# Experts in the order of their token counts, three of them as 64 slots with high and low halves side by side

## Chip, cores, metric

One core of a Trainium2 chip runs the whole program. The metric is the device time of one execution in microseconds (us); the runs of the kernel before give a median.

## What is computed

Two layers of a hybrid trunk on 256 latent tokens and 256 context tokens, then a final norm. The change lies in the second layer's expert part alone:

```python
logits = (x @ router_w).astype(F32)
top_val, top_idx = lax.top_k(logits, TOP_K)          # 2 of 8 experts
gates = jax.nn.softmax(top_val, axis=-1)
def swiglu(x, w1, w3, w2):
    return (jax.nn.silu(x @ w1) * (x @ w3)) @ w2
y = jax.ops.segment_sum(yb * buf_gate[:, None].astype(yb.dtype), buf_tok, num_segments=n_tok + 1)
```

256 tokens choose two experts each, so 512 rows are spread over 8 experts of width 1024 to 2816 to 1024, all in fp32. With the inputs used here the reference's router gives experts 0 to 7 the counts 46, 68, 65, 64, 79, 75, 55 and 60.

## The kernel before

`stage_two` holds the expert part. A token's slot within an expert is the number of tokens before it with the same expert (`rank`). `place` builds for every expert the 0/1 matrix `G` (256 tokens by 128 slots), `gather` multiplies the tokens' rows by it for a pair of experts, `back` transposes it into `GT`, and `scatter` brings an expert's rows back to their tokens and adds them to `xlat`. If an expert had more than 128 tokens (`nmax > P`), the whole loop `experts` would run once more on the rest.

`experts` goes through the experts 0 to 7. Each has 33 weight chunks of 1 MB (128 partitions by 2048 values): 22 for w1 and w3 (two for each of 11 steps `b`), 11 for w2. `raws` gives a chunk one of nine places of its own (`NQ + NX`) and, for two early ones, a place borrowed from another tile; SP's queue issues the loads in the order of the program and waits for a place to come free. `wsplit` makes two fp32r halves out of a chunk: ScalarE (ACT) casts it to the high part `wh` (L1056), VectorE (DVE) subtracts to get the low part `wl` (L1057), 1024 columns at a time, into four places each (`NSW`). An fp32 product is then three fp32r products on TensorE (PE):

```python
pe.matmul(p, xh, wH, start=(kt == 0), stop=False)
pe.matmul(p, xh, wL, start=False, stop=False)
pe.matmul(p, xl, wH, start=False, stop=(kt == KT - 1))
```

(L1203 to L1205 for w1 and w3, the same in L1253 to L1255 for w2), each with 128 slots as the stationary operand and 512 weight columns streaming: 12 a chunk. After a step's 24 products ACT takes the silu (L1213), DVE multiplies (L1214), PE transposes two tiles of 128x128 (L1217), and ACT and DVE split the result into `gh` and `gl` (L1223, L1224). Two PSUM banks `h` take turns between steps. At the end of a half of w2, ACT and DVE scale and split the rows (L1258, L1259).

The order of instructions on each engine is fixed when the program is built, by a scheduler that moves them away from the order of the code; at run time every engine goes through its own list and waits where an operand is missing.

## Time and profile before

| | us |
|---|---|
| median of 3 runs | 1838.36 |
| lowest, highest run | 1838.15, 1841.06 |
| span of the profiled execution, first to last instruction | 1837.7 |
| TensorE busy in it | 1776.0 (97%) |
| VectorE busy | 1413.4 (77%) |
| ScalarE busy | 1058.8 (58%) |
| mean rate of the DMA engines | 223 GB/s |

The profiled execution's own time is its span, 1837.7 us, and what lies around the span, which the profile does not hold. A busy time is the union of an engine's instructions; a share over the whole span averages stages of different kinds, and the expert loop is the last 800 us or so. Pipelined products overlap in the records, so the distance from one start to the next tells more than one record's length.

### The profile page before, as it was taken

How to read it: one execution, taken by the hardware profiler on the slowest of the kernel's cores; microseconds unless marked ns; L12 is line 12 of the kernel's file. 1: busy time of each engine (PE TensorE's matmuls, PEld its weight loads, DVE VectorE, ACT ScalarE, POOL GpSimd, SP SyncE). 2: the span in 40 equal slices, each digit the busy share in tenths (PEclk: the TensorE clock that was granted, in tenths of full speed). 3: DMA queues.
4: the chain of work that ended last, by engine and by line, in shares of the span. 5: the costliest groups of instructions: out<-in, count | busy, mean ns of one | idle time of the engine just before them, and what ended most of it. 6: DMA issues, size and time to landing. Idle time of an engine off the chain costs nothing.

```text
span 1837.7 us, 24441 instructions
## 1 busy us (share of the span) xinstructions
PE 1776.0 (97%) x8925; PEld 1403.1 (76%) x8925; DVE 1413.4 (77%) x2437; ACT 1058.8 (58%) x1648; POOL 3.0 (0%) x9
## 2 busy tenths in 40 slices
PE   6999999999999999899999899999999999999997
PEld 4776666778888888687768788888787878878786
DVE  4657757679986333677767899999889998999896
ACT  3455556533222222365456687878777777777775
POOL 0000000000000000000000000000000000000000
PEclk9999999989999999899999899999999999999998
DMA  9643211227785332331315789989998999989991
GB/s 302 224 143 126 81 45 51 72 93 241 232 309 204 92 97 78 125 101 55 104 50 184 290 332 354 367 333 354 341 345 334 353 346 346 358 330 367 341 368 61
DMA packets 82863, 410.09 MB, mean 223 GB/s; under 512 B 8912, under 2 KB 18640, under 8 KB 48944
## 3 DMA queue, kind: packets, MB, share of 16 engines
q1 hardware_dynamic: 82000, 406.62, 61.8%
q8 instruction: 72, 1.18, 0.3%
q0 software_dynamic: 304, 1.29, 0.2%
q10 hardware_dynamic: 432, 0.55, 0.1%
q14 instruction: 55, 0.45, 0.1%
HBM read 407.38 MB, written 1.05 MB: 222 GB/s over the span
## 4 chain that ended last, share of the span: by engine, by line
PE 91%; DVE 3%; ACT 2%; DMA 2%; issue 1%; SPq 0%; DVEq 0%; ACTq 0%; POOLq 0%
PE ah L1204 9%; PE ah L1203 9%; PE ah L1205 9%; PE ay L1254 4%; PE ay L1255 4%; PE ay L1253 4%; PE atr L1217 1%; PE axgp L1164 1%; DMA aw<-ada 1%; PE asc L1267 1%; PE nk L87 1%; PE nk L85 1%; PE cq L85 1%; PE nk L86 1%; PE cq L87 1%
## 5 line engine op out<-in xcount | busy, mean ns | idle before, releaser
L1057 DVE TENSOR_TENSOR am_1wl<-am_1w,am_1wh 128x1024 fp32r<-128x1024 f32 (+1 forms) x178 | 210.9, 1210 | 25.2 <-ACT am_1wh L1056 21.6
L1057 DVE TENSOR_TENSOR am_0wl<-am_0w,am_0wh 128x1024 fp32r<-128x1024 f32 (+1 forms) x178 | 209.8, 1206 | 3.8 <-ACT am_0wh L1056 3.2
L1056 ACT CAST am_0wh<-am_0w 128x1024 fp32r<-128x1024 f32 (+1 forms) x178 | 180.2, 1044 | 15.3 <-PE ah L1205 8.1
L1056 ACT CAST am_1wh<-am_1w 128x1024 fp32r<-128x1024 f32 (+1 forms) x178 | 179.1, 1036 | 9.1 <-PE ah L1205 7.7
L1205 PE MATMUL ah<-am_0wh,axl 128*128 128x512 f32 x352 | 142.5, 405 | 0.0
L1204 PE MATMUL ah<-am_0wl,axh 128*128 128x512 f32 x352 | 140.5, 399 | 0.0
L1203 PE MATMUL ah<-am_0wh,axh 128*128 128x512 f32 x352 | 139.4, 396 | 0.0
L1204 PE MATMUL ah<-am_1wl,axh 128*128 128x512 f32 x352 | 138.7, 394 | 0.0
L1203 PE MATMUL ah<-am_1wh,axh 128*128 128x512 f32 x352 | 138.0, 392 | 0.0
L1205 PE MATMUL ah<-am_1wh,axl 128*128 128x512 f32 x352 | 137.5, 391 | 0.0
L249 DVE CUSTOM_DVE_ANT_0 junk<-awr,crow,sp 128x1024 f32<-128x1024 f32 x80 | 102.6, 1283 | 12.9 <-DMA awr<-adr 11.6
L1213 ACT ACTIVATE as<-ah 128x256 f32<-128x256 f32 x88 | 34.0, 386 | 88.2 <-PE ah L1205 88.2
L1203 PEld LDWEIGHTS ah<-am_1wh,axh 128*128 128x128 f32 x352 | 66.1, 188 | 14.8
L1205 PEld LDWEIGHTS ah<-am_1wh,axl 128*128 128x128 f32 x352 | 66.1, 188 | 13.8
L1204 PEld LDWEIGHTS ah<-am_1wl,axh 128*128 128x128 f32 x352 | 66.2, 188 | 13.7 <-DVE am_1wl L1057 0.4
L1204 PEld LDWEIGHTS ah<-am_0wl,axh 128*128 128x128 f32 x352 | 66.4, 189 | 13.2 <-DVE am_0wl L1057 0.9
L1203 PEld LDWEIGHTS ah<-am_0wh,axh 128*128 128x128 f32 x352 | 66.6, 189 | 12.5 <-ACT axh L1169 0.4
L1205 PEld LDWEIGHTS ah<-am_0wh,axl 128*128 128x128 f32 x352 | 66.4, 189 | 11.3
L1214 DVE TENSOR_TENSOR as<-as,ah 128x256 f32<-128x256 f32 x88 | 36.4, 414 | 4.6 <-ACT as L1213 4.6
L1224 DVE TENSOR_TENSOR agl<-atr,agh 128x256 fp32r<-128x256 f32 x88 | 36.8, 418 | 1.9 <-ACT agh L1223 1.2
L1223 ACT CAST agh<-atr 128x256 fp32r<-128x256 f32 x88 | 32.7, 372 | 5.5 <-PE atr L1217 5.1
L1217 PEld LDWEIGHTS atr<-ck,as 128*128 128x128 f32 x176 | 23.5, 139 | 13.7 <-DVE as L1214 4.3
(6122 smaller groups left out, 4884.8 us busy)
## 6 DMA issues: line engine op xcount, KB each, us to landing
am_0w<-m SPq DMA_DIRECT2D x88, 1024.0 KB, 5.7
am_1w<-m SPq DMA_DIRECT2D x88, 1024.0 KB, 6.1
awr<-adr SPq DMA_DIRECT2D x56, 512.0 KB, 4.5
aw<-ada SPq DMA_DIRECT2D x24, 512.0 KB, 4.6
aw<-ada SPq DMA_DIRECT2D x32, 256.0 KB, 6.0
av_0w<-m SPq DMA_DIRECT2D x8, 1024.0 KB, 5.4
av_1w<-m SPq DMA_DIRECT2D x8, 1024.0 KB, 5.8
av_2w<-m SPq DMA_DIRECT2D x8, 1024.0 KB, 5.0
```

The lines of the kernel that those rows point to most:

```text
L85: pe.matmul(ps, a[0], b[0], start=first, stop=False)
L249: ins = dve.tensor_tensor_reduce(out=junk, in0=w, in1=rows[v], op0=OP.mult, op1=OP.add, scale=1.0, scalar=sp[:, l, b:b + 1], accum_out=mod ...
L1056: act.copy(h[:, c], r)
L1057: dve.tensor_tensor(l[:, c], r, f32(h[:, c]), op=OP.subtract)
L1203: pe.matmul(p, xh, wH, start=(kt == 0), stop=False)
L1204: pe.matmul(p, xh, wL, start=False, stop=False)
L1205: pe.matmul(p, xl, wH, start=False, stop=(kt == KT - 1))
L1217: pe.transpose(tr[:, u * P:(u + 1) * P], s[:, u * P:(u + 1) * P], ident)
L1224: dve.tensor_tensor(gl, trv, f32(gh), op=OP.subtract)
L1253: pe.matmul(yq, gh, wH, start=(f == 0), stop=False)
L1254: pe.matmul(yq, gh, wL, start=False, stop=False)
L1255: pe.matmul(yq, gl, wH, start=False, stop=(f == NF - 1))
```

## The change

The program counts the tokens of each expert on the chip (`order`), ranks experts 1 to 7 by count and visits them in an order of eight places: place 0 stays expert 0, places 1, 3 and 5 get those with the three smallest counts (`RANKS`). SP reads the seven numbers into registers (`values_load`), and the loads of places 1 to 7 take their address from one (`weights`). `G`, gates and ranks are permuted to places.

Places 1, 3 and 5 (`NARROW`) hold at most 64 tokens. Their stationary tile has the 64 tokens' high parts in columns 0 to 63 and the low parts in columns 64 to 127, so two products (by `wH` and `wL`) do what three did (`narrow`). Of their 33 chunks, five (`WHOLE`) are not split: one plain fp32 product streams the raw chunk. A step's result then has the high parts' sums in partitions 0 to 63 and the low parts' in 64 to 127: ACT copies the bank out (`ev`) and a product with `fold` adds the lower half to the upper. Silu, multiplication and transposes go over 64 partitions or columns. Experts are gathered as 0, then 1 and 2, 3 and 4, 5 and 6, then 7. The gates' arithmetic is called at the same place; `place` for the others comes after `order`. A second pass runs if a place overflows its cap of 64 or 128.

```diff
@@ -49,8 +49,14 @@
-C_ID, C_ONE, C_IOTA, C_SEL, C_TIE = 0, 128, 256, 384, 392
-N_CK = 456
+C_ID, C_ONE, C_IOTA, C_SEL, C_TIE, C_SIG = 0, 128, 256, 384, 392, 456
+N_CK = 488
+RANKS = (0, 1, 4, 2, 5, 3, 6, 7)
+NARROW = (1, 3, 5)
+CAP = tuple(64 if s in NARROW else 128 for s in range(8))
+WHOLE = (3, 10, 16, 23, 29)
 T_R, T_M0, T_M1, T_UP, T_LO, T_BO, T_K = 0, 512, 896, 1280, 1408, 1536, 1664
...
@@ -1039,12 +1045,14 @@
-        def wsplit(src, name):
+        def wsplit(src, name, split=True):
             rt_ = raws(nchunk[0], name + "w")
...
             nchunk[0] += 1
+            if not split:
+                return [(rt_[0][:, :1024], None), (rt_[0][:, 1024:], None)]
             res = []
...
@@ -1058,20 +1066,29 @@
         def unit(ws, k, c0=0, n=512):
-            return [t[:, k % 2 * 512 + c0:k % 2 * 512 + c0 + n] for t in ws[k // 2]]
+            return [t if t is None else t[:, k % 2 * 512 + c0:k % 2 * 512 + c0 + n] for t in ws[k // 2]]
+        def narrow(p, x, w, first, last):
+            if w[1] is None:
+                pe.matmul(p, f32(x), w[0], start=first, stop=last)
+            else:
+                pe.matmul(p, x, w[0], start=first, stop=False)
+                pe.matmul(p, x, w[1], start=False, stop=last)
...
         oh1, oh2, asg, gate, rank, rk2, t1 = (rt[:, i] for i in range(7))
+        asgp, rankp, gatep = oh1, oh2, t1
         lg = plog
...
@@ -1111,26 +1128,25 @@
-        def place(rk, e0, e1):
+        def place(rk, ag, e0, e1, nm):
             for e in range(e0, e1):
                 for tt in range(2):
-                    ins = dve.tensor_scalar(G[tt][:, e, :], iota, rk[:, tt, e:e + 1], asg[:, tt, e:e + 1],
+                    g = G[tt][:, e, :]
+                    i = iota
+                    if nm == "a" and e in NARROW:
+                        g = g.rearrange("p (a b) -> p a b", a=2)
+                        i = ck[:, None, C_IOTA:C_IOTA + 64].to_broadcast([P, 2, 64])
+                    ins = dve.tensor_scalar(g, i, rk[:, tt, e:e + 1], ag[:, tt, e:e + 1],
                                             op0=OP.is_equal, op1=OP.mult)
...
-        with tc.issue_after(place(rank, 0, 2).ins):
+        with tc.issue_after(place(rank, asg, 0, 1, "a").ins):
             for p_ in parts[HL:]:
...
         def gates():
...
@@ -1144,82 +1160,157 @@
             dve.tensor_tensor(gate, gate, t1, op=OP.add)
-            dve.tensor_scalar(rk2, rank, -128.0, None, op0=OP.add)
-            return ci
-        cnti = []
+        def order():
...
+            for tt in range(2):
+                pe.matmul(pr[:, 16:24], on, lot[:, tt, :], start=(tt == 0), stop=(tt == 1))
+            dve.tensor_copy(cnt, pr[:, 16:24])
+            dve.tensor_tensor(key, cnt, row[0], op=OP.mult)
+            dve.tensor_tensor(key, key, row[1], op=OP.add)
+            dve.tensor_tensor(w1_, key[:, None, :].to_broadcast(sq8), key[:, :, None].to_broadcast(sq8), op=OP.is_lt)
+            dve.tensor_reduce(pos, w1_, AX.X, OP.add)
+            dve.tensor_tensor(hot, pos[:, None, :].to_broadcast(sq8), row[2][:, :, None].to_broadcast(sq8), op=OP.is_equal)
+            dve.tensor_tensor(w1_, hot, i8[:, None, :].to_broadcast(sq8), op=OP.mult)
+            dve.tensor_reduce(idx, w1_, AX.X, OP.add)
+            dve.tensor_copy(oi[:, :NEXP], idx)
...
+            for dst, src in ((rankp, rank), (asgp, asg), (gatep, gate)):
+                by_place(dst, src)
+            dve.tensor_tensor(w1_, hot, cnt[:, None, :].to_broadcast(sq8), op=OP.mult)
+            dve.tensor_reduce(over, w1_, AX.X, OP.add)
...
+            fold = whole.tile([P, P], F32R, tag="before", name="fold")
+            dve.tensor_copy(fold[:, :64], ident[:, 64:])
+            dve.tensor_scalar(fold[:, 64:], ident[:, :64], 0.0, None, op0=OP.mult)
+            return oi, fold
+        oi, regs = [], []
         def experts(rk, nm):
...
+            def gather(e0, ne):
...
+                            if e0 + i in thin:
+                                dve.scalar_tensor_tensor(h_[:, m:c], pv[:, m:c], sh, f32(h_[:, a:m]), op0=OP.add,
+                                                         op1=OP.subtract)
...
             def slots(e):
-                if e == 0 and nm == "a":
-                    cnti.append(gates())
                 pg = bank("t", 2, f"{nm}pg{e}")
                 for tt in range(2):
-                    pe.matmul(pg[:, :1], f32(G[tt][:, e, :]), gate[:, tt, e:e + 1], start=(tt == 0), stop=(tt == 1))
+                    pe.matmul(pg[:, :1], f32(G[tt][:, e, :]), gatep[:, tt, e:e + 1], start=(tt == 0), stop=(tt == 1))
                 dve.tensor_copy(gs[:, e:e + 1], pg[:, :1])
...
                 tr = bank("t", 2, f"{nm}gt{e}")
-                for u in range(2):
-                    for tt in range(2):
-                        pe.transpose(tr[:, u * NL + tt * P:u * NL + (tt + 1) * P], f32(G[tt][:, e + u, :]), ident)
-                act.copy(GT[:, e:e + 2, :], tr.rearrange("p (e t) -> p e t", e=2))
+                for tt in range(2):
+                    pe.transpose(tr[:, tt * P:(tt + 1) * P], f32(G[tt][:, e, :]), ident)
+                act.copy(GT[:, e, :], tr[:, :NL])
+            def weights(key, e, *c):
+                return I[key][(e, *c)] if e == 0 else I[key][(bass.ds(regs[e], 1), *c)].rearrange("o p c -> (o p) c")
...
                 if e == 0:
-                    xg = gather(0)
-                    place(rk, 2, NEXP)
-                o = (e % 2) * P
+                    xg = gather(0, 1)
+                o = 0 if e == 0 else (e - 1) % 2 * P
+                slim = e in thin
+                n_ = 64 if slim else P
                 gts = []
...
                     for kh in range(2):
-                        ws = wsplit(I["m13"][e, b, kh], f"{nm}m{e}_{b}_{kh}")
+                        ws = wsplit(weights("m13", e, b, kh), f"{nm}m{e}_{b}_{kh}", not (slim and 2 * b + kh in WHOLE))
                         for k4 in range(4):
...
                             xh, xl = xg[0][:, kt, o:o + P], xg[1][:, kt, o:o + P]
+                            if slim:
+                                narrow(p, xh, (wH, wL), kt == 0, kt == KT - 1)
+                                continue
                             pe.matmul(p, xh, wH, start=(kt == 0), stop=False)
...
                             pe.matmul(p, xl, wH, start=False, stop=(kt == KT - 1))
-                    if b == SLB:
+                    if slim:
+                        ev = cp.tile([P, 512], F32, tag="pm", bufs=3, name=f"{nm}ev{e}_{b}").bitcast(F32R)
+                        act.copy(ev, p)
+                        pe.matmul(p, oi[1], ev, start=False, stop=True, skip_group_check=True)
+                    if nm == "a" and e == 0 and b == SLB:
+                        gates()
+                        oi.extend(order())
+                        regs.extend([0] + [nc.values_load(oi[0][0:1, s_:s_ + 1], engines=[mybir.EngineType.SP], min_val=0,
+                                                          max_val=NEXP - 1) for s_ in range(1, NEXP)])
+                    if nm == "a" and e == 0 and b == SLB + 1:
+                        place(rankp, asgp, 1, NEXP, nm)
+                    if b == SLB + 1:
                         slots(e)
-                    if e == 0 and BK <= b < BK + 4:
-                        back(2 * b - 2 * BK)
+                    if b == BK:
+                        back(e)
                     if b == 1 and late:
                         late.pop()()
-                    s = cp.tile([P, 512], F32, tag="pm", bufs=3, name=f"{nm}s{e}_{b}")[:, :256]
-                    act.activation(s, p[:, :256], AF.Silu)
-                    dve.tensor_tensor(s, s, p[:, 256:], op=OP.mult)
+                    s = cp.tile([P, 512], F32, tag="pm", bufs=3, name=f"{nm}s{e}_{b}")[:n_, :256]
+                    act.activation(s, p[:n_, :256], AF.Silu)
+                    dve.tensor_tensor(s, s, p[:n_, 256:], op=OP.mult)
...
+                    if slim:
+                        act.copy(gh[:, :, :64], trv)
+                        dve.tensor_tensor(gh[:, :, 64:], trv, f32(gh[:, :, :64]), op=OP.subtract)
+                        gts.append((gh, None))
+                        continue
...
@@ -1227,16 +1318,16 @@
                     hh, f = divmod(u, NF)
-                    if u == 16 and e % 2 == 1 and e + 1 < NEXP:
-                        xg = gather((e + 1) // 2)
+                    if u == 16 and e % 2 == 0 and e + 1 < NEXP:
+                        xg = gather(e + 1, min(2, NEXP - 1 - e))
                     if u % 4 == 0:
-                        ws = wsplit(I["m2"][e, u // 4], f"{nm}v{e}_{u // 4}")
+                        ws = wsplit(weights("m2", e, u // 4), f"{nm}v{e}_{u // 4}", not (slim and 22 + u // 4 in WHOLE))
                     if e == NEXP - 1 and u == NF:
...
@@ -1248,8 +1339,11 @@
                             f = u_ % NF
+                            wH, wL = unit(ws, u_ % 4, q * n, n)
+                            if slim:
+                                narrow(yq, gts[f // 2][0][:, f % 2, :], (wH, wL), f == 0, f == NF - 1)
+                                continue
                             gh, gl = gts[f // 2][0][:, f % 2, :], gts[f // 2][1][:, f % 2, :]
-                            wH, wL = unit(ws, u_ % 4, q * n, n)
                             pe.matmul(yq, gh, wH, start=(f == 0), stop=False)
...
@@ -1304,8 +1398,8 @@
         experts(rank, "a")
-        nmax = nc.values_load(cnti[0][0:1, 0:1], min_val=0, max_val=NL)
-        with tc.If(nmax > P):
+        nmax = nc.values_load(oi[0][0:1, NEXP:NEXP + 1], min_val=0, max_val=NL)
+        with tc.If(nmax > 0):
             experts(rk2, "b")
...
@@ -1320,6 +1414,7 @@
     ck[:, C_TIE:C_TIE + NEXP * NEXP] = np.where(e[None] < e[:, None], 0, np.where(e[None] > e[:, None], 1.2e-38, 3.0e38)).ravel()
+    ck[:, C_SIG:C_SIG + 32] = np.concatenate([[0] + [8] * 7, [-1, 1, 2, 3, 4, 5, 6, 7], RANKS, CAP])[None]
     ck[:, C_SEL:C_SEL + 8] = (i[:, None] % 32) == np.arange(8)[None]
```

How the built order moves is seen at two places. The first is PE in the first of the three places (`ah` is a step's bank, the number behind it the step; `wh`, `wl` the weights' parts; `aev` the copied bank; `atr` the transposes). Before, in the second expert, the nine products that follow step 2's last one and its two gate products, and then the transposes of step 2:

```order
L1203 MATMUL ah_3_9796<-am_3_0wh_9799,axh_8643 128x512
L1204 MATMUL ah_3_9796<-am_3_0wl_9800,axh_8643 128x512
L1205 MATMUL ah_3_9796<-am_3_0wh_9799,axl_8644 128x512
L1203 MATMUL ah_3_9796<-am_3_0wh_9799,axh_8643 128x512
L1204 MATMUL ah_3_9796<-am_3_0wl_9800,axh_8643 128x512
L1205 MATMUL ah_3_9796<-am_3_0wh_9799,axl_8644 128x512
L1203 MATMUL ah_3_9796<-am_3_0wh_9803,axh_8643 128x512
L1204 MATMUL ah_3_9796<-am_3_0wl_9804,axh_8643 128x512
L1205 MATMUL ah_3_9796<-am_3_0wh_9803,axl_8644 128x512
L1217 MATMUL atr_2_9791<-ck,as_2_9788 128x128 x2
```

Now, from the last product of step 2 on:

```order
L1079 MATMUL ah_2_9850<-am_2_1wl_9876,axh_9516 128x512
L1078 MATMUL ah_3_9898<-am_3_0wh_9901,axh_9516 128x512
L1079 MATMUL ah_3_9898<-am_3_0wl_9902,axh_9516 128x512
L1078 MATMUL ah_3_9898<-am_3_0wh_9901,axh_9516 128x512
L1079 MATMUL ah_3_9898<-am_3_0wl_9902,axh_9516 128x512
L1078 MATMUL ah_3_9898<-am_3_0wh_9905,axh_9516 128x512
L1079 MATMUL ah_3_9898<-am_3_0wl_9906,axh_9516 128x512
L1078 MATMUL ah_3_9898<-am_3_0wh_9905,axh_9516 128x512
L1283 MATMUL ah_2_9850<-aev_2_9887,fold 128x512
L1079 MATMUL ah_3_9898<-am_3_0wl_9906,axh_9516 128x512
L1078 MATMUL ah_3_9898<-am_3_1wh_9919,axh_9516 128x512
```

Two products stand where three stood, the fold of step 2 comes seven products after its last one, and the transposes of step 2 (two of 128x64) eight products after the fold.

The second place is DVE in the first expert, step 3 to step 4 (`am_3_1wl` and `am_4_0wl` are low parts of the chunks of steps 3 and 4, `ordw` the work area of `order`, `oi` the numbers for SP). Before:

```order
L1057 TENSOR_TENSOR am_3_1wl_8928<-am_3_1w,am_3_1wh_8927 128x1024
L1146 TENSOR_TENSOR rt<-rt 128x16
L1214 TENSOR_TENSOR as_2_8894<-as_2_8894,ah_2_8825 128x256
L1180 COPY gslot<-apg_8890 128x1
L1057 TENSOR_TENSOR am_3_1wl_8932<-am_3_1w,am_3_1wh_8931 128x1024
L1057 TENSOR_TENSOR am_4_0wl_8959<-am_4_0w,am_4_0wh_8958 128x1024
L1224 TENSOR_TENSOR agl_0_8769<-atr_2_8897,agh_0_8768 128x256
L1057 TENSOR_TENSOR am_4_0wl_8963<-am_4_0w,am_4_0wh_8962 128x1024
```

Now, from the last split of step 3:

```order
L1065 TENSOR_TENSOR am_3_1wl_9006<-am_3_1w,am_3_1wh_9005 128x1024
L1183 TENSOR_TENSOR ordw<-ordw,ck 128x64
L1315 TENSOR_TENSOR agl_0_8755<-atr_2_8971,agh_0_8754 128x256
L1184 TENSOR_TENSOR ordw<-ordw,ck 128x64
L1190 TENSOR_TENSOR ordw<-ordw,rt 128x128
L1185 TENSOR_REDUCE ordw<-ordw 128x8
L1191 TENSOR_REDUCE rt<-ordw 128x16
L1186 CAST oi<-ordw 128x8
L1195 TENSOR_TENSOR ordw<-ordw 128x64
L1190 TENSOR_TENSOR ordw<-ordw,rt 128x128
L1196 TENSOR_REDUCE ordw<-ordw 128x8
L1191 TENSOR_REDUCE rt<-ordw 128x16
```

Before, two splits of successive chunks stand side by side there. Now 34 instructions stand between the last split of step 3 and the first of step 4: 17 of `order`, 14 that build `G` for the other seven experts (these stood ahead of step 1 before), the copy of the gates and two that stood there before too.

## Rows read from the trace of the kernel before

**Rows 1.** The page: span, and busy time of each engine.

```profile
span 1837.7 us, 24441 instructions
PE 1776.0 (97%) x8925; PEld 1403.1 (76%) x8925; DVE 1413.4 (77%) x2437; ACT 1058.8 (58%) x1648; POOL 3.0 (0%) x9
```

**Rows 2.** The page: the chain that ended last, by line.

```profile
PE ah L1204 9%; PE ah L1203 9%; PE ah L1205 9%; PE ay L1254 4%; PE ay L1255 4%; PE ay L1253 4%; PE atr L1217 1%; PE axgp L1164 1%; DMA aw<-ada 1%; PE asc L1267 1%; PE nk L87 1%; PE nk L85 1%; PE cq L85 1%; PE nk L86 1%; PE cq L87 1%
```

**Rows 3.** The chain in time: one place, two experts apart (start us, us, what).

```profile
1304.81 0.47 PE ay L1253 x2
...
1504.91 0.47 PE ay L1253 x2
```

**Rows 4.** Busy time by stretch: those two experts.

```profile
core 0: us, PE busy (x) PEld busy (x) DVE busy (x) ACT busy (x) POOL busy (x), PEclk, DMA share, GB/s
...
1304.80:1504.90 200.10, 197.46 (x910) 160.46 (x909) 181.04 (x207) 147.98 (x188) 0.00 (x0) 1.00 0.94 346
```

**Rows 5.** Waits in those two experts: us in total, times, longest.

```profile
PE ay L1254 <- DVE av_7wl L1057: 2.4, 2, 1.2
...
PEld atr L1217 <- DVE as L1214: 0.6, 1, 0.6
```

**Rows 6.** Timeline of PE, two products twelve apart (start us, us).

```profile
1170.44 0.39 PE L1203 MATMUL ah<-am_1wh,axh 128*128 128x512 f32 x1
...
1173.19 0.39 PE L1203 MATMUL ah<-am_0wh,axh 128*128 128x512 f32 x1
```

**Rows 7.** Plain fp32 products of 512 columns: one tile's row, one of the chain.

```profile
L772 PE MATMUL krr<-krs,ctB x2: 587/588/588, 863.1 to 863.5; 64*128 64x512 f32 x2
...
915.86 0.86 PE ma1010s L376 x2
```

**Rows 8.** The chain: four transposes of 128 columns.

```profile
1081.46 0.44 PE agt L1186 x4
```

**Rows 9.** Groups by line and shape, those two experts, DVE.

```profile
L1057 DVE TENSOR_TENSOR am_1wl<-am_1w,am_1wh 128x1024 fp32r<-128x1024 f32 x44 | 52.1, 1221 | 8.1 <-ACT am_1wh L1056 8.1
...
L1224 DVE TENSOR_TENSOR agl<-atr,agh 128x256 fp32r<-128x256 f32 x22 | 9.2, 418 | 0.2 <-ACT agh L1223 0.2
L1214 DVE TENSOR_TENSOR as<-as,ah 128x256 f32<-128x256 f32 x22 | 9.1, 414 | 2.0 <-ACT as L1213 2.0
```

**Rows 10.** The same for ACT.

```profile
L1056 ACT CAST am_0wh<-am_0w 128x1024 fp32r<-128x1024 f32 x44 | 44.3, 1055 | 1.4 <-PE ay L1255 1.4
...
L1213 ACT ACTIVATE as<-ah 128x256 f32<-128x256 f32 x22 | 8.5, 386 | 31.7 <-PE ah L1205 31.7
L1223 ACT CAST agh<-atr 128x256 fp32r<-128x256 f32 x22 | 8.2, 374 | 0.9 <-PE atr L1217 0.9
...
L1258 ACT ACTIVATE ayy<-ay,gslot 128x512 fp32r<-128x512 f32 x4 | 2.8, 689 | 6.2 <-PE ay L1255 6.2
```

**Rows 11.** Timeline of DVE: small instructions at the routing, and two splits.

```profile
1019.88 0.29 DVE L1081 TENSOR_REDUCE rt<-duel 128x16 f32<-128x128 f32 x1
1020.20 0.17 DVE L1083 TENSOR_SCALAR lot<-rt 128x16 bf16<-128x16 f32 x1
...
1021.92 1.11 DVE L1117 TENSOR_SCALAR G<-ck,rt 128x128 fp32r<-128x128 f32 x4
...
1041.26 2.35 DVE L1057 TENSOR_TENSOR am_1wl<-am_1w,am_1wh 128x1024 fp32r<-128x1024 f32 x2
```

**Rows 12.** SP's reading of a number into a register: length ns min/median/max.

```profile
L1307 SPq TENSOR_LOAD <-cnti x1: 484/484/484, 1792.6 to 1792.6; - x1
L1307 SPq FUSED_REGOPS  x1: 182/182/182, 1793.1 to 1793.1; - x1
L1307 SPq SEQ_ASSERT  x1: 32/32/32, 1793.3 to 1793.3; - x1
```

**Rows 13.** Busy time by stretch: first loads of the experts, and full flow.

```profile
1000.00:1005.00 5.00, 5.00 (x47) 4.93 (x46) 3.65 (x9) 4.11 (x16) 0.00 (x0) 1.00 1.00 419
...
1255.00:1290.00 35.00, 35.00 (x161) 28.36 (x160) 32.89 (x37) 28.84 (x37) 0.00 (x0) 1.00 1.00 367
```

60 lines of the change are left out of this document (41 added, 19 removed).

## The prediction

> **What bounds the kernel now.** Read the page first: TensorE (PE) is busy for 1776.0 of 1837.7 us [rows 1], and the chain that ended last is mostly the expert loop's products [rows 2]. That is an average over the program, so the next view is the chain in time: the same place in the list of work comes at 1304.81 and at 1504.91, two experts apart [rows 3]. An expert thus takes 100.05 us, and this stage alone is changed. In those 200 us PE is busy 197.46, VectorE (DVE) 181.04, ScalarE (ACT) 147.98, and the granted clock is 1.00, the upper of the two levels, 2.4 GHz [rows 4]. PE waited 2.4 us for a split and 0.6 us for the multiplication ahead of a transpose [rows 5]. So PE sets the pace, but per expert DVE needs 90.5 us (half of 181.04) and ACT 74.0: whatever is taken from PE soon meets DVE.
>
> **A place with 64 slots, on PE.** Two products twelve apart start at 1170.44 and 1173.19 [rows 6]: 0.229 us each, 2.75 us for a chunk of twelve.
> - 28 chunks lose four of twelve products: 28 x 4 x 0.229 = 25.7 us gone.
> - Five chunks go through in plain fp32. The trace has such products of 512 columns: one product shows as two records (the rotary key's tile is written by one product and has two), and the pair takes 0.86 us [rows 7]. Four of these are 3.44 us against 2.75 for the twelve they replace: 5 x 0.69 = 3.5 us added.
> - Eleven folds of 512 columns: 11 x 0.229 = 2.5 us added.
> - 22 transposes stream 64 columns instead of 128. Four of 128 take 0.44 us [rows 8]; half of 0.11 us is saved on each, 1.2 us, and nothing if a short one is no faster.
>
> Together 25.7 - 3.5 - 2.5 + 1.2 = 20.9 us less, so 79.2 us a place if PE never waits; for three places 62.7 us.
>
> **The same place on DVE and ACT.** Five unsplit chunks drop ten subtractions. Two in a row take 2.35 us and one alone 1.22 [rows 9, 11], so one more costs 1.13 us: 11.3 us less. The subtraction that makes the low part of the hidden values (L1224, 418 ns) goes over 128 elements instead of 256; by the 1.13 us of 1024 elements that is 0.14 us less, 1.5 for eleven. DVE falls from 90.5 to 77.7 us. ACT drops ten casts of 1.05 us, gains eleven copies of 128x512 at about the 0.69 us of L1258, and halves L1223 (374 ns): 74.0 - 10.5 + 7.6 - 1 = 70 us [rows 10]. DVE would be busy 98% of PE's 79.2 us where it is now at 90%. The four places for split halves let it run ahead by two chunks, and PE's 3.44 us on an unsplit chunk let it catch up.
>
> **Waits inside a step.** The fold is a new link: last product, copy on ACT, fold on PE, silu, multiplication, transposes. In the built order seven products (1.60 us) stand between last product and fold. The copy needs at most the product's tail of 0.16 (0.39 less 0.23), the rest of a cast of 1.05 and its own 0.69: 1.90 us, so PE waits 0 to 0.30. From the fold to the transposes there are eight products (1.83 us) for the fold's 0.39, a cast's rest, the silu of 0.39, a subtraction's rest of 1.22 and the multiplication of 0.41: 3.46 us, so 0 to 1.63 [rows 6, 9, 10]. Over eleven steps that is 0 to 21.2 us a place. Today's shorter chain stands at its low end, 0.6 us in 200 [rows 5], but with DVE some 10% idle. I take a quarter of the bound, 5 us, as both engines lie closer to PE: 84.2 us a place. Against 100.05 that saves 15.9 us, for three places 47.6.
>
> **The first expert.** Before step 4's first split DVE now has 32 more instructions. Six on 128 elements cost 0.32 us each, fourteen of `G` 0.28 (four in 1.11), seven small ones about 0.2 [rows 11], and five on 64 elements 0.25, my value between: 1.9 + 3.9 + 1.4 + 1.3 = 8.5 us. Meanwhile PE still has six products of step 3 (1.4 us) and 16 products of the next gather, some 1.9 us, which it would otherwise do later. So it stands still for about 5 us. On the other side, the 3.9 us of `G` no longer stand ahead of the first splits, while ten instructions of the gates (2 us) do: the first expert starts about 2 us earlier. Net 3 us lost; the ends are 2 us won and 8.5 lost.
>
> **SP and the loads.** Seven readings of 0.484 + 0.182 + 0.032 us are 4.9 us [rows 12], and SP first waits for `oi`; the loads of the last five w1/w3 chunks of the first expert and all later ones queue behind. Eighteen loads are issued by then, while DVE is at the ninth chunk, so nine chunks (25 us of products) cover it; uncovered it would cost up to 4.9 us. A register in an address adds one instruction to a load, against 2.5 us between loads. I cost both at nothing.
>
> **Transfers.** A chunk is 1.049 MB, and 33 in 84.2 us are 411 GB/s, more than today's 346 [rows 4]. When the first nine chunks are all queued, 419 GB/s arrive; in full flow, where a load is issued only as DVE frees a place, 367 at a share of 1.00 [rows 13]. I take it that the smaller number is the demand. Even at 367 (2.86 us a chunk) the five experts from place 1 to 5, of whose 165 chunks nine are ahead, need 156 x 2.86 + 5 for the last chunk = 451 us, where the forecast has 3 x 84.2 + 2 x 100.05 = 452.7. So this rate just covers it.
> The Trainium skill, page "DMA: Bandwidth & Descriptors", section "Where 436 GB/s comes from", has HBM bind a core's loads at about 358 GB/s. The 419 GB/s of rows 13 disagree; by the page the sum would be about 1803 us (first rival).
>
> **Sum.** 1837.7 - 47.6 + 3 = 1793.1 us of span. The median of the runs lies 0.7 above the span (1838.36), so **1794 us**.
>
> **Rivals.**
> 1. *Transfers set the pace.* For it: the DMA engines' share is already 0.94 over two whole experts [rows 4]. Against it: the 419 GB/s. If no more than today's mean 346 GB/s comes, 3.03 us a chunk, places 1 to 5 take 156 x 3.03 + 5 = 478 us instead of 500.25: 22.6 us gained, 1837.7 - 22.6 + 3 + 0.7 = 1819 us. By the page's 358 it would be 2.93 us a chunk, 462 us, 1803 us.
> 2. *The step's chain becomes the bound, slower than before.* Place: fold and transposes of each of 33 steps. At the full bound PE loses 3 x 21.2 = 63.6 of the 62.7 us, and with 8.5 us in the first expert it ends at 1848 us. It decides from a mean wait of (62.7 - 3)/33 = 1.8 us a step. For it: ACT and DVE are at 88 and 98% of PE's time, so an instruction often arrives behind another. Against it: the bound asks that each of three links meets a fresh cast or split, and two banks `h` let the next step go on. Halfway, 10.6 us a place, gives 1810 us.
> 3. *No waits at all.* The scheduler's order fits and only PE counts: 1837.7 - 62.7 + 3 + 0.7 = 1779 us. Against it: DVE at 98%.
> 4. *The change doesn't fit the data.* Counts of experts 1 to 7 are 68, 65, 64, 79, 75, 55, 60; the three smallest, 55, 60 and 64, just fit 64 slots. One token more and the second pass adds about eight experts of 100 us: 2594 us. It decides at a count of 65; the closest of the 256 tokens' second and third logits differ by 0.005 of a mean size of 2.5, far from rounding.
>
> **How the numbers follow.** A measurement of this kernel tells about 0.2%, 3.7 us, from no change. The forecast's case, 1785 to 1806 us, has 0.58. Rival 1 has 0.15 and rival 3 0.12; rival 2 has 0.07 for its half-way value and 0.05 for its end above 1842; 0.02 stays for within 0.2%, and 0.01 for the second pass. Faster: 0.58 + 0.15 + 0.12 + 0.07 = 0.92; same 0.02; slower 0.06. The range goes from rival 3 with a slightly better first expert, 1777, to rival 1's upper end, 1818.
>
> **What would show it.** Places 1, 3 and 5 should each take 82 to 88 us and the other experts about 100. In the three places: fp32 products as pairs of records 0.43 us apart, DVE busy over 90%, PE's waits behind `ev`, silu and splits adding to about 5 us a place. In the first expert: a pause of PE of 3 to 7 us near step 4. SP should wait for DVE, not DVE for loads, and GB/s should rise over 380 in the narrow places. If products there wait for loads, rival 1 holds; if transposes or folds wait over 1 us each, rival 2; if a second pass runs, rival 4. I am wrong if a narrow place takes over 93 us or under 80.

## The result, and the profile after

The changed kernel takes 1829.09 us (median of 4 runs, 1828.04 to 1829.72) against 1838.92 us before: a ratio of 0.9946, 95% interval 0.9932 to 0.9960. It is faster, by 9.8 us; the prediction had 44 us and a range that ended at 1818.

First the page of the changed kernel: span, busy times, and the chain by line.

```profile
span 1826.2 us, 24297 instructions
...
PE 1754.1 (96%) x8594; PEld 1333.9 (73%) x8594; DVE 1376.5 (75%) x2460; ACT 1037.5 (57%) x1661; POOL 3.0 (0%) x9
...
PE ah L1278 6%; PE ah L1277 5%; PE ah L1279 5%; DVE am_1wl L1065 2%; PE ay L1348 2%; PE ah L1079 2%; PE ay L1349 2%; PE ay L1347 2%; PE ay L1079 1%; PE ah L1078 1%; PE ah L1076 1%; PE ay L1078 1%; ACT am_1wh L1064 1%; PE ay L1076 1%; PE axgp L1224 1%
```

Against [rows 1, 2]: PE is busy 22 us less, and in the chain that ended last two lines are new that are not PE's, the split (L1065, 2%) and the cast (L1064, 1%). So there are stretches in which PE waits for them. The next view puts them in their places. A place is counted from the second scaling of `y` on ACT (L1352) to the next place's.

Busy time by stretch, changed kernel, places 1 to 5 (1, 3 and 5 are the narrow ones):

```profile
core 0: us, PE busy (x) PEld busy (x) DVE busy (x) ACT busy (x) POOL busy (x), PEclk, DMA share, GB/s
1131.40:1214.30 82.90, 82.04 (x320) 54.48 (x320) 74.55 (x89) 66.18 (x91) 0.00 (x0) 1.00 0.97 392
1214.30:1315.80 101.50, 101.19 (x474) 82.24 (x473) 93.36 (x116) 75.76 (x99) 0.00 (x0) 1.00 0.96 360
1315.80:1411.70 95.90, 89.62 (x320) 53.64 (x320) 75.53 (x89) 68.12 (x93) 0.00 (x0) 1.00 0.90 343
1411.70:1513.20 101.50, 101.19 (x473) 82.22 (x472) 93.33 (x116) 75.74 (x100) 0.00 (x0) 1.00 0.95 360
1513.20:1609.10 95.90, 89.61 (x320) 53.64 (x319) 75.53 (x89) 68.12 (x92) 0.00 (x0) 1.00 0.90 342
```

This table is the whole case. The first narrow place takes 82.9 us; 84.2 was forecast. The other two, with the same instructions, take 95.9 us each, 13 us more. DVE and ACT work nearly the same time in all three (74.6 to 75.5 and 66.2 to 68.1 us), so hardly anything there became slower: in places 3 and 5 all the engines have gaps, and so have the transfers (share 0.90).

What PE waits for in place 3 (us in total, times, longest), changed kernel. PEld is PE's loading of a product's stationary operand, which comes ahead of the product and waits with it:

```profile
PE ah L1079 <- DVE am_1wl L1065: 4.0, 9, 0.6
...
PEld ah L1079 <- DVE am_1wl L1065: 12.1, 20, 1.0
PEld ah L1283 <- ACT aev L1282: 5.0, 11, 0.9
PEld atr L1302 <- DVE as L1299: 4.4, 10, 0.8
```

In place 1 the first of these is 0.2 us, and the second and third are 1.5 and 2.0. So PE waits above all at the second chunk of a step (`am_1`) for its low part, and less at the fold for ACT's copy and at the transposes for the multiplication. One step of place 3 shows how the two hang together. The timelines of PE, ACT and DVE (start, us long, instruction):

```profile
1340.09 0.39 PE L1079 MATMUL ah<-am_1wl,axh 128*128 128x512 f32 x1
...
1341.16 0.50 PE L1283 MATMUL ah<-aev,fold 128*128 128x512 f32 x1
...
1343.36 0.39 PE L1078 MATMUL ah<-am_1wh,axh 128*128 128x512 f32 x1
1344.32 0.50 PE L1079 MATMUL ah<-am_1wl,axh 128*128 128x512 f32 x1 [0.57 <-DVE am_1wl L1065]
```

```profile
1340.52 0.59 ACT L1282 CAST aev<-ah 128x512 fp32r<-128x512 f32 x1 [0.43 <-PE ah L1079]
1341.70 0.38 ACT L1298 ACTIVATE as<-ah 64x256 f32<-64x256 f32 x1 [0.59 <-PE ah L1283]
1341.98 1.03 ACT L1064 CAST am_1wh<-am_1w 128x1024 fp32r<-128x1024 f32 x1
```

```profile
1342.11 0.41 DVE L1299 TENSOR_TENSOR as<-as,ah 64x256 f32<-64x256 f32 x1 [0.30 <-ACT as L1298]
1343.04 1.23 DVE L1065 TENSOR_TENSOR am_1wl<-am_1w,am_1wh 128x1024 fp32r<-128x1024 f32 x1 [0.52 <-ACT am_1wh L1064]
```

Read it as one line: last product of a step at 1340.09, copy 1340.52, fold 1341.16, silu 1341.70, then the cast of the next step's second chunk 1341.98, its split 1343.04, the product that needs it 1344.32. That is 4.2 us from last product to that product, and PE has only the step's first chunk (1.83 us), the fold and two transposes to fill it. The cast and the split don't need the silu; they merely stand behind it on their engines. The built order says so. DVE, step 2 to step 3, first in place 1 and then in place 3 (`as_2` is the multiplication of step 2):

```
L1065 TENSOR_TENSOR am_3_1wl_9920<-am_3_1w,am_3_1wh_9919 128x1024
L1065 TENSOR_TENSOR am_3_1wl_9924<-am_3_1w,am_3_1wh_9923 128x1024
L1299 TENSOR_TENSOR as_2_9890<-as_2_9890,ah_2_9850 64x256
```

```
L1065 TENSOR_TENSOR am_3_0wl_11554<-am_3_0w,am_3_0wh_11553 128x1024
L1299 TENSOR_TENSOR as_2_11538<-as_2_11538,ah_2_11498 64x256
L1065 TENSOR_TENSOR am_3_1wl_11568<-am_3_1w,am_3_1wh_11567 128x1024
```

In place 1 all four half-chunk splits of step 3 stand ahead of step 2's multiplication, in places 3 and 5 two. The fold stands seven products behind step 2's last one in place 1, two in places 3 and 5. The other steps of the built order show which of the two counts. In place 1 the fold comes one to seven products behind, at step 1 just one; but the casts of the next step stand ahead of the silu at every step but the last, where one of four is missing. In places 3 and 5 the fold comes one or two products behind at every step, and at every step from the second on two of the next step's casts and splits stand behind the silu and the multiplication.

### The profile page after: what moved, and what is told of

Read it like the earlier page. It is cut to its first block, busy times and chain, and to the rows that moved or that the text cites. A ratio compares the mean times of both kernels' runs of the same rounds, so it can differ in the third digit from the quotient of the medians.

```text
span 1826.2 us, 24297 instructions
## 1 busy us (share of the span) xinstructions
PE 1754.1 (96%) x8594; PEld 1333.9 (73%) x8594; DVE 1376.5 (75%) x2460; ACT 1037.5 (57%) x1661; POOL 3.0 (0%) x9
## 4 chain that ended last, share of the span: by engine, by line
PE 87%; DVE 7%; ACT 3%; issue 1%; DMA 1%; SPq 0%; ACTq 0%; DVEq 0%; POOLq 0%
PE ah L1278 6%; PE ah L1277 5%; PE ah L1279 5%; DVE am_1wl L1065 2%; PE ay L1348 2%; PE ah L1079 2%; PE ay L1349 2%; PE ay L1347 2%; PE ay L1079 1%; PE ah L1078 1%; PE ah L1076 1%; PE ay L1078 1%; ACT am_1wh L1064 1%; PE ay L1076 1%; PE axgp L1224 1%
## 5 line engine op out<-in xcount | busy, mean ns | idle before, releaser
L1065 DVE TENSOR_TENSOR am_1wl<-am_1w,am_1wh 128x1024 fp32r<-128x1024 f32 (+1 forms) x172 | 203.6, 1208 | 30.4 <-ACT am_1wh L1064 29.7
L1065 DVE TENSOR_TENSOR am_0wl<-am_0w,am_0wh 128x1024 fp32r<-128x1024 f32 (+1 forms) x166 | 194.4, 1205 | 9.2 <-ACT am_0wh L1064 9.0
L1064 ACT CAST am_1wh<-am_1w 128x1024 fp32r<-128x1024 f32 (+1 forms) x172 | 172.7, 1035 | 5.4 <-PE ah L1279 2.7
L1064 ACT CAST am_0wh<-am_0w 128x1024 fp32r<-128x1024 f32 (+1 forms) x166 | 166.1, 1041 | 10.5 <-PE ah L1279 6.4
L1279 PE MATMUL ah<-am_0wh,axl 128*128 128x512 f32 x220 | 90.0, 409 | 0.0
L1277 PE MATMUL ah<-am_0wh,axh 128*128 128x512 f32 x220 | 87.7, 398 | 0.0
L1279 PE MATMUL ah<-am_1wh,axl 128*128 128x512 f32 x220 | 85.9, 391 | 0.0
L1298 ACT ACTIVATE as<-ah 128x256 f32<-128x256 f32 (+1 forms) x88 | 33.7, 383 | 78.6 <-PE ah L1279 63.4
L1299 DVE TENSOR_TENSOR as<-as,ah 128x256 f32<-128x256 f32 (+1 forms) x88 | 36.5, 414 | 27.4 <-ACT as L1298 27.1
L1278 PEld LDWEIGHTS ah<-am_0wl,axh 128*128 128x128 f32 x220 | 41.9, 191 | 10.7 <-DVE am_0wl L1065 3.0
L1277 PEld LDWEIGHTS ah<-am_1wh,axh 128*128 128x128 f32 x220 | 41.3, 188 | 9.5
L1277 PEld LDWEIGHTS ah<-am_0wh,axh 128*128 128x128 f32 x220 | 42.0, 191 | 7.8
L1278 PEld LDWEIGHTS ah<-am_1wl,axh 128*128 128x128 f32 x220 | 41.3, 188 | 8.4 <-DVE am_1wl L1065 0.2
L1279 PEld LDWEIGHTS ah<-am_1wh,axl 128*128 128x128 f32 x220 | 41.4, 188 | 8.1
```

Source lines behind the costliest of these rows:

```text
L1064: act.copy(h[:, c], r)
L1065: dve.tensor_tensor(l[:, c], r, f32(h[:, c]), op=OP.subtract)
```

## Theories and experiments

Theory A: the built order of places 3 and 5 puts copy, fold, silu, cast and split in one row on PE's path. Theory B: the transfers set the pace. B has a number on its side: the prediction's first rival, at 346 GB/s, gave 478 us for places 1 to 5, and they took 1609.1 - 1131.4 = 477.7. Against B speak three rows of the changed kernel in place 3, a load on SP, its cast on ACT, and SP's largest wait:

```profile
1358.35 0.33 SPq L1052 DMA_DIRECT2D av_0w<-m  x1
```

```profile
1381.94 2.00 ACT L1064 CAST av_0wh<-av_0w 128x1024 fp32r<-128x1024 f32 x2
```

```profile
SPq L1052 <- DVE am_1wl L1065: 27.9, 9, 4.0
```

This load was issued 23.6 us ahead of its use and landed in 4.9, and SP waits for DVE to free places; no engine has a wait for a load among its rows there. But a wait that no row names isn't excluded by that, so it was tried.

**Forced order.** In the narrow places the next step's splits are written ahead of the fold, and copy, silu and multiplication may only follow them:

```diff
...
+                        if b + 1 < NFB:
+                            ahead.update({(b + 1, kh): chunk(b + 1, kh) for kh in range(2)})
+                            for ins in lastcast:
+                                hold.enter_context(tc.issue_after(ins.ins))
                         ev = cp.tile(...)
...
```

> All arithmetic is kept; in the three narrow places every step's copy, silu and multiplication are made to stand behind the splits of the whole next step on ACT and DVE. In the changed kernel the first narrow place has four half-chunk splits ahead of a step's multiplication and takes 82.9 us; the other two have two ahead and take 95.9 us each. Theory A (the order on ACT, DVE and PE puts the chain copy, fold, silu, split on PE's path in those two): both fall to 82 to 87 us, and the whole to about 1829 - 2 x 11 = 1807 us (1800 to 1812). Theory B (transfers set the pace, 350 GB/s over places 3 and 4): no place gets shorter by more than 2 us, 1825 to 1832 us.

Measured: 1819.89 us, ratio to before 0.9898 (0.9881 to 0.9914). Neither theory's number. Place 3 of it:

```profile
1318.60:1409.40 90.80, 86.10 (x320) 53.60 (x319) 75.65 (x89) 67.11 (x93) 0.00 (x0) 1.00 0.94 361
```

**No fold.**

```diff
-                        act.copy(ev, p)
-                        pe.matmul(p, oi[1], ev, start=False, stop=True, skip_group_check=True)
```

> Leaves out the copy of the bank and the fold, so the low parts of the tokens are not added in the narrow places. The order still has two half-chunk splits ahead in places 3 and 5 (one in their first step). Theory A: a step's chain loses the copy of 0.59 us and the fold with its start, about 1.1 us, eleven times in each of two places: 95.9 falls to about 83 us, the whole to 1800 to 1808 us. Theory B (transfers): the loads are the same, so 95.9 stays and the whole is 1825 to 1830 us.

Measured: 1817.45 us, 0.9885 (0.9866 to 0.9905); again neither theory's number. Place 3:

```profile
1314.50:1405.30 90.80, 84.93 (x309) 50.84 (x308) 75.23 (x89) 61.97 (x81) 0.00 (x0) 1.00 0.95 360
```

Two different cuts into the chain, and both came to 90.8 us at 360 GB/s. This looks like B with a better rate, and it is why the next run was needed. The waits, though, are not alike. ACT's largest in place 3, with the forced order and without the fold:

```profile
ACT as L1307 <- PE ah L1292: 11.7, 11, 1.9
```

```profile
ACT agh L1305 <- PE atr L1298: 11.7, 11, 2.0
```

With the forced order ACT stands at the silu for a fold that comes nine or ten products behind at most steps; without the fold it stands at the copy behind the transposes, with casts queued behind it.

**The order written out.** In the narrow places every instruction of PE, ACT and DVE in a step follows the one before it by a dependency: a half-chunk is split as soon as its place is free, the fold comes behind seven products, the transposes behind fifteen (fewer in a step with an unsplit chunk). Parts of the edit:

```diff
...
+                            if b and j == 1 and i == len(ops) - 1:
+                                (s_tr if kh else s_fold)(b - 1)
+                            link("p", pe.matmul(p, x_, w_, start=(kt == 0), stop=last))
+                        if b and j == 1:
+                            (s_gh if kh else s_mul)(b - 1)
+                        if lds:
+                            nx[kh].append(half(lds[kh], j, link))
...
```

> All arithmetic is kept; in the three narrow places the order on PE, ACT and DVE is written out: per step, each half-chunk's split stands right behind the products that free its place, the fold behind seven products of the next step, the multiplication ahead of the splits of the next step's second half, the transposes behind fifteen products. Full loads. Theory A (only the order holds the second and third narrow places up): all three take 81 to 85 us and the whole is about 1820 - 2 x 8 = 1804 us (1798 to 1808). Theory B (transfers hold what the forced order left: both kernels that shortened the chain in different ways came to 90.8 us in those two places at 360 GB/s): they stay at 90 to 92 us, and the whole at 1817 to 1822 us.

Measured: 1805.89 us (1805.23 to 1807.83), 0.9823 (0.9806 to 0.9839). Places 1, 3 and 5:

```profile
1133.40:1215.60 82.20, 81.25 (x320) 54.97 (x319) 74.82 (x89) 66.07 (x92) 0.00 (x0) 1.00 0.98 395
...
1317.10:1401.40 84.30, 81.91 (x320) 54.68 (x319) 75.36 (x89) 67.08 (x92) 0.00 (x0) 1.00 0.97 392
...
1502.90:1587.20 84.30, 81.94 (x320) 54.67 (x319) 75.37 (x89) 67.08 (x93) 0.00 (x0) 1.00 0.97 390
```

Theory A holds and B falls: the same bytes arrive at 390 GB/s as soon as the order asks for them. The order alone was worth 1829.09 - 1805.89 = 23.2 us, more than twice what the change itself brought; in the profiles it is 0.7 in place 1 and 11.6 in each of places 3 and 5.

**Half loads.** Two runs ask what the transfers still cost, and where the bad order comes from. Each load brings half a chunk, and both halves are cut from what it brought, in the changed kernel and in the one with the written order (`lds` of a narrow place likewise). Half of the weights are left out by that, so these two tell about time alone:

```diff
-                nc.sync.dma_start(raw, src[:, i * w:i * w + w])
+                nc.sync.dma_start(raw[:, :w // 2], src[:, i * w:i * w + w // 2])
...
```

> Every load of an expert's weights brings half of the bytes, and both halves of a chunk use the loaded half (so half of the weights are left out). With it the built order changes: four half-chunk splits stand ahead of a step's multiplication in all three narrow places, as only in the first of the changed kernel. Theory A: all three narrow places take what the first takes now, 82 to 84 us, the wide ones stay at 98 to 101, and the whole is about 1829 - 26 = 1803 us. Theory B (transfers): the narrow places go on down to PE's own work, 77 to 80 us, the first too, and the whole to below 1798 us.

Measured: 1798.90 us (0.9785, 0.9765 to 0.9804), narrow places 81.6, 81.6 and 81.7 us, between the two theories' numbers. Place 3:

```profile
1312.20:1393.80 81.60, 81.06 (x321) 54.80 (x320) 74.33 (x89) 66.70 (x92) 0.00 (x0) 1.00 0.64 207
```

The builder gave all three narrow places nearly the order that place 1 has in the changed kernel (three or four of four splits ahead), although nothing but the loads and where the halves are read was changed. So the order follows from the loads as the builder reckons them. That it reckons with those of places 3 and 5 later than they come would fit the early load shown above, but was not shown.

> The written order with loads of half the bytes; both halves of a chunk use the loaded half, so half of the weights are left out. With full loads the three narrow places take 82.2, 84.3 and 84.3 us at 390 to 395 GB/s. If transfers no longer cost anything there, all three stay within 0.5 us of 82 to 84; if the 2.1 us between the first and the others is loads that come late, the second and third fall to 82.2 as well, and the whole to about 1801 us.

Measured: 1796.05 us (0.9768, 0.9749 to 0.9788). Its place 3:

```profile
1313.20:1393.50 80.30, 79.88 (x320) 55.16 (x319) 74.29 (x89) 66.77 (x92) 0.00 (x0) 1.00 0.66 210
```

All three are at 80.3 or 80.4, further down than either case expected. So full loads cost 2 us in place 1 and 4 in the others, together with the order at a place's first step and in w2, which isn't written out and which the builder changed here too. PE is busy for 79.9 us of the 80.3, next to no wait; the prediction had 79.2 for a place without waits.

**Ordering alone.** `NARROW = ()`: sorting, readings, addresses and gathers as changed, three products everywhere.

> Experts are ordered on chip and their weights addressed by registers, but no place is narrow: three products everywhere. What the ordering alone costs: by the trace of the changed kernel PE stands still for 1.9 us at 1050 to 1060 us and the end behind the last output is 2.3 us longer, so 1841 to 1845 us. If register addresses or the readings delayed loads, the wide places would take over 101.5 us on average and the whole would pass 1848 us; if the ordering is hidden, 1838 to 1840 us.

Measured: 1849.72 us, 1.0062 (1.0046 to 1.0079): the ordering costs 11.1 us, far from the 3 that were forecast. The expectation put a time over 1848 us down to late loads, with places of over 101.5 us on average; places 1 to 7 take 99.6, so that isn't the cause. In the profiles, 8.1 us of it lie between the first ranking product and the end of place 0, 0.8 in places 1 to 7 and 1.9 behind them. Against it, the narrow places bring 1849.72 - 1829.09 = 20.6 us as built and 43.8 with the written order.

**The gathers.** The kernel before, with five gathers in place of four:

```diff
-                    xg = gather(0)
+                    xg = gather(0, 1)
...
-                    if u == 16 and e % 2 == 1 and e + 1 < NEXP:
-                        xg = gather((e + 1) // 2)
+                    if u == 16 and e % 2 == 0 and e + 1 < NEXP:
+                        xg = gather(e + 1, min(2, NEXP - 1 - e))
```

> The kernel before with nothing changed but the gathers: expert 0 alone, then pairs (1,2), (3,4), (5,6), then 7 alone, five gathers instead of four. If a product of 128 columns takes half of one of 256, the columns are the same and the time is that of before, 1837 to 1840 us. If it takes as long (0.112 us against 0.118 us by the trace of the changed kernel), one gather of 32 products is added, 3.7 us: 1841 to 1844 us, and the rest of the 11 us that the ordering alone costs belongs to the sorting, its readings and the clock.

Measured: 1843.18 us, 1.0019 (1.0009 to 1.0029), 4.1 us more. In the changed kernel, gather products of 128 columns (pairs) and of 256:

```profile
1687.59 0.39 PE L1224 MATMUL axgp<-G,hH 128*128 128x128 f32 x2
1687.81 0.38 PE L1224 MATMUL axgp<-G,hL 128*128 128x128 f32 x2
...
1108.76 0.40 PE L1224 MATMUL axgp<-G,hH 128*128 128x256 f32 x2
1109.00 0.41 PE L1224 MATMUL axgp<-G,hL 128*128 128x256 f32 x2
```

A pair takes 0.22 us with 128 columns and 0.24 with 256. For PE, gathering one expert is nearly as dear as gathering two. The 4.1 us (1.7 to 5.3 by the interval) are a balance: by the profiles the first expert, which now holds a second gather, takes 6.7 us more and places 1 to 7 together 3.2 less.

**The register.** SP reads none of the seven expert numbers into registers; each place's expert is a number in the program, the one that the sorting finds:

```diff
-                return ... I[key][(bass.ds(regs[e], 1), *c)].rearrange("o p c -> (o p) c")
+                return I[key][((0, 6, 2, 7, 1, 3, 5, 4)[e] if nm == "a" else e, *c)]
```

> The kernel with the written order, but SP reads no registers: each place's expert is written into the program as the number that the sorting gives for this data, and the loads have fixed addresses (the sorting itself still runs). If seven readings and an address by register cost nothing, as the prediction had it: 1805 to 1807 us as with them. If the loads behind the readings come late and PE waits for them: 2 to 5 us less, 1801 to 1804 us.

Measured: 1802.16 us (1802.01 to 1806.40), 0.9803 (0.9790 to 0.9816). The number is that of the expectation's second case, but not its cause: the expert loop is the same to the tenth, 82.2, 84.3, 84.3 us in the narrow places, so no load comes late. The time lies around it. The last scaling of the last place and the span, with the written order, and then without registers:

```profile
span 1804.3 us, 24282 instructions
...
1786.99 0.47 ACT L1452 ACTIVATE ayy<-ay71b,gslot 128x256 fp32r<-128x256 f32 x1 [0.94 <-PE ay71b L1449]
```

```profile
span 1800.3 us, 23797 instructions
...
1784.82 0.47 ACT L1450 ACTIVATE ayy<-ay71b,gslot 128x256 fp32r<-128x256 f32 x1 [0.94 <-PE ay71b L1447]
```

The end is 17.3 us with registers and 15.5 without; before it is 1837.7 - 1822.35 = 15.4. So the readings and the addresses by register cost 1.8 us, not in the loads but at the program's end, behind the branch that skips the second pass. There SP works through eight semaphore instructions of the branch's line (L1502, L1500 without registers); the fifth starts 1.9 us after the fourth with registers, and 0.1 us after it without. Why wasn't found out. The other 2 us are ahead of the experts: the first ranking product starts at 1019.43 us with registers and at 1017.23 without, and between 1016.2 and 1020.5 us in the profiles of this study, whatever the kernel.

**G spread out.** Over the written order, `place` for one expert behind each of seven steps instead of all seven at once.

> The kernel with the written order, and the 14 instructions that build the other seven places' columns of G are spread over seven steps of the first expert, two behind each, instead of 14 in one piece behind the sorting. If DVE's block of 34 instructions is what makes PE stand still for 1.6 to 1.9 us at 1050 to 1060 us, the first expert gets 1.5 to 2.5 us shorter, and the whole as much; if the block is covered anyway, no change within 1 us.

Measured: 1805.12 us (1804.68 to 1809.69), 0.9825 (0.9809 to 0.9841): not to be told from 1805.89. PE still waits 0.7 us in front of the first transposes there, where it waited 1.0. In the profile the first expert is 1.9 us shorter, but that can't be put to the spreading: with the written order alone PE's granted clock drops again after the pause at the sorting (0.80 and 0.85 in the two stretches of 5 us from 1055 us on), and in this profile it stays at 1.00.

**How many chunks in plain fp32.** Three runs with the written order; the third also with `G` spread. They have `WHOLE = ()`, then `(3, 7, 11, 15, 19, 23, 27, 31)`, then `(3, 11, 19, 27)`.

> The kernel with the written order, and no chunk of the narrow places in plain fp32: all 33 are split and go through as two products. PE loses 5 x 0.69 = 3.5 us of work a place, DVE gets ten more splits, 11.3 us, on the 75.4 us that it is busy in 84.3. If DVE is then the bound, a place takes 87 to 91 us and the whole 1814 to 1826 us; if PE's work alone counted, a place would take 80 to 82 us and the whole 1797 to 1802.

> The written order with eight chunks in plain fp32 instead of five (every fourth, from the fourth on). PE gets 3 x 0.69 = 2.1 us more a place, DVE 6.8 us less. If PE sets the pace at five already, a place takes 2 to 3 us longer and the whole 1811 to 1815 us; if DVE still sets it, a place gets shorter and the whole falls below 1805.

> The written order with G spread over seven steps, and four chunks in plain fp32 instead of five (every eighth, from the fourth on). Against a split chunk of two products an unsplit one costs PE 3.44 - 1.83 = 1.6 us, and spares DVE 2.3. With none a narrow place took 87.5 us (DVE busy 84.8), with five 84.3, with eight 88.9 (PE busy 86.3). PE would have 81.9 - 1.6 = 80.3 us and DVE 75.4 + 2.3 = 77.7 a place: if PE's work still sets the pace, 82.7 us a place and the whole 1800 to 1803 us; if loads do (392 GB/s), 84 and 1804 to 1807 us.

Measured: 1815.91 us (0.9873, 0.9857 to 0.9890), 1820.45 (0.9905, 0.9888 to 0.9921) and 1818.21 (0.9885, 0.9869 to 0.9900). Place 3 with none, with eight and with four:

```profile
1320.50:1408.00 87.50, 78.34 (x320) 52.87 (x319) 84.81 (x99) 76.68 (x103) 0.00 (x0) 1.00 0.98 384
```

```profile
1320.50:1409.40 88.90, 86.30 (x320) 54.90 (x319) 69.59 (x83) 62.71 (x87) 0.00 (x0) 1.00 0.96 380
```

```profile
1316.40:1404.40 88.00, 82.85 (x320) 53.63 (x318) 76.74 (x90) 69.34 (x94) 0.00 (x0) 1.00 0.97 379
```

With none DVE is busy 97% and sets the pace; with eight PE is, 97%. The expectation of the second run was mis-sized: against the eight products of a split chunk (1.83 us) an unsplit one (3.44 us) costs PE 1.6 us, not 0.69. Three times that is 4.8, near what place 3 lost (88.9 - 84.3 = 4.6), but the fit proves little, as the third run shows. It missed both its cases: four chunks took 88.0 us, 3.7 more than five, with PE busy 94% and DVE 87%. No count of work explains that; the places in the row of chunks were others too. The traces show a part: in place 3 of this run PE waits 1.5 and 0.7 us for the splits of w2's chunks 7 and 1, which are two of the five unsplit chunks of the kernel with five. The run with none has both waits, that with eight the first. The rest stays open, and with it what the number of chunks alone is worth.

## Why the prediction was wrong

**The bound, and PE's work in a narrow place: right, in part by luck.** 79.2 us was forecast, and 80.3, with PE busy 79.9, is what it came to with next to no waits, in the written order with half loads. But the 100.05 us from which 20.9 were taken are the mean of an expert with a gather and one without. The narrow places have none: with the ordering alone, places 3 and 5 take 98.7 us, and from there to 80.3 are 18.4, not 20.9. The piece that was wrong is the short transposes, which were to save 1.2 us or nothing. In the changed kernel, a pair of 64 columns and then one of 128, each with the product ahead and the second one behind:

```profile
1169.41 0.40 PE L1078 MATMUL ah<-am_1wh,axh 128*128 128x512 f32 x1
1169.74 0.33 PE L1302 MATMUL atr<-ck,as 64*128 64x64 f32 x2
...
1170.35 0.39 PE L1078 MATMUL ah<-am_1wh,axh 128*128 128x512 f32 x1
```

```profile
1258.97 0.40 PE L1278 MATMUL ah<-am_0wl,axh 128*128 128x512 f32 x1
1259.20 0.38 PE L1302 MATMUL atr<-ck,as 128*128 128x128 f32 x2
...
1259.65 0.39 PE L1277 MATMUL ah<-am_0wh,axh 128*128 128x512 f32 x1
```

From the product ahead to the second one behind it is 0.94 us with the short pair and 0.68 with the long one. Two products without a pair take 0.46, so a short pair costs 0.48 us and a long one 0.22: eleven pairs cost some 2.9 us more, where 1.2 less were forecast.

**DVE and ACT: nearly right.** 77.7 and 70 us were forecast, 75.5 and 68.1 measured in place 3.

**Waits inside a step: this failed.** The step is the sentence "In the built order seven products (1.60 us) stand between last product and fold", with the quarter of a bound that was built on it. It holds for step 2 of the first narrow place, from which it was read, and was taken for every step of all three. Already in that place it is one to seven products; the place still takes 82.9 us against 84.2, as the next step's casts stand ahead of the silu there. In places 3 and 5 one or two products stand there, two casts and splits fewer are ahead, and the place takes 95.9 us: 16.0 over PE's 79.9 where 5 were forecast, and 11.6 over the same place with the written order. That is within the bound of 21.2, but by another wait. The bound has the chain held up by casts and splits, and puts a price on the fold and the transposes. What PE mostly waits for (12.1 us in PEld's row above, against 5.0 at the fold and 4.4 at the transposes) is the split of the next step's second chunk, whose cast was held up by the chain; for that the sum has no term. With the written order in all three places the saving is 43.8 us against the 47.6 of the prediction.

**The first expert and the ordering: mis-sized.** Forecast 3 us, measured 11.1. Of these 4.1 are the fifth gather, which the sum doesn't have; 1.8 are the registers at the end, costed at nothing; PE's waits at the sorting are these, from 1050 to 1060 us of the changed kernel:

```profile
PE atr L1302 <- DVE as L1299: 1.0, 1, 1.0
PE ah L1278 <- DVE am_0wl L1065: 0.6, 1, 0.6
PE apg L1247 <- DVE ordw L1199: 0.2, 1, 0.2
```

That is 1.9 us by the unrounded gaps, where 5 were forecast. DVE's block took 6.6 us (from 1049.38 to 1055.96) and not 8.5; the gather of the next pair, which the forecast had counted, fills most of the rest. And the clock stayed low for longer. Busy time by stretch, before and then changed:

```profile
1025.00:1030.00 5.00, 5.00 (x28) 4.43 (x28) 3.57 (x12) 2.27 (x5) 0.00 (x0) 0.71 0.02 8
1030.00:1035.00 5.00, 5.00 (x25) 4.16 (x24) 4.91 (x11) 4.57 (x7) 0.00 (x0) 1.00 0.00 0
```

```profile
1025.00:1030.00 5.00, 5.00 (x18) 4.42 (x18) 1.40 (x4) 1.92 (x5) 0.00 (x0) 0.50 0.09 34
1030.00:1035.00 5.00, 5.00 (x20) 3.98 (x20) 3.09 (x3) 3.35 (x4) 0.00 (x0) 0.85 0.00 0
```

In both PE stood still for over 6 us at the ranking (5.13 and 1.17 us, with three small products between), and its clock was then 0.50, the level of 1.2 GHz. Before, it is back at 2.4 GHz from 1028 us on, behind 16 gather products and four of 512 columns (0.43 us each); now PE runs 32 gather products and eleven of 512 columns ahead of that, until 1031 us. The run of the gathers alone shows the same (0.50 from 1025 to 1030 us, 0.70 in the next 5), so its 4.1 us hold this cost. Of the 11.1 us, 11.1 - 4.1 - 1.8 - 1.9 = 3.3 are left, no more than the intervals of these runs allow. The profiles put them into places 1 to 7, which take 696.9 us together with the ordering alone and 693.0 with the gathers alone. Each place there now does the transposes of its own `G`, which before were all in the first expert; what that costs wasn't measured by itself.

**SP and the loads, transfers: right in kind.** SP waited for DVE and not the reverse, and readings and addresses cost the loop nothing. Full loads do cost 2 to 4 us a narrow place once the order no longer does, with what hangs on the order of its first step and of w2; they were costed at nothing.

**The sum.** 1829.1 - 1794 = 35.1 us: 23.2 from the order, nearly all of it in places 3 and 5, 8.1 from the ordering (11.1 - 3), 3.8 from the saving (47.6 - 43.8).

**The rivals.** The second came nearest: the step's chain did become the bound, in two places and almost not in the first, while it had been weighed as one case for all three. But its own sign, transposes or folds that wait over 1 us each, didn't come: they wait 0.5 us or less on average, and the longest 0.9. The prediction's other sign did, a narrow place over 93 us. The first rival had the right number, 477.7 against 478 us for places 1 to 5, by a mechanism that the written order refutes. A number that fits is no evidence for its cause.

## What to carry to other kernels

Where a program orders the instructions, read the order at every place and every step where the changed code stands, not at the first: the same loop body can come out well once and badly twice. Wherever a fresh link (copy, fold) is put on an in-order engine, look at what queues behind it; here casts and splits that didn't need the silu stood behind it, and writing out the order of a step, for all steps of the three places, won 23 us without one instruction less. And price a product that gets narrower by a row with that width, since a narrow one may take as long as a wide one.

## What the hardware showed

- At a granted clock of 1.00 a product of fp32r with 128 columns takes 0.11 us, with 256 columns 0.12 and with 512 columns 0.23 [rows 6]; between such products, a pair of transposes of 64 columns costs 0.48 us and one of 128 columns 0.22.
- Loads sustained 390 to 395 GB/s over a whole narrow place of 82 to 84 us. The Trainium skill, page "DMA: Bandwidth & Descriptors", section "Where 436 GB/s comes from", has HBM bind a core at about 358 GB/s, half of what a stack gives to two cores; here one core was at work, and the runs lie above it.
- SP's first register reading took 0.47 us, about as the one before did [rows 12], the six after it 0.26 or 0.27 each.
